# Layer A of a hybrid conv/attention trunk: a staging tile in two buffers, one column copied on another engine, one running sum begun without a copy

## The chip, the cores and the metric

The kernel runs on one core of one Trainium2 chip. The metric is the device time of one execution in microseconds; the time given for a kernel is the median of several runs. The engines of the core are TensorE (PE, with its weight loads shown as PEld), VectorE (DVE), ScalarE (ACT), GpSimd (POOL) and SyncE (SP, which issues the DMAs here). Each works through its own queue in order and waits for the others by semaphores.

## What is computed

Two layers over 1024 tokens of width 1024, in fp32, with 256 memory tokens. Layer A, which the change touches, mixes by a causal convolution of 31 taps over 1536 channels with a layer norm over the channels; layer B mixes by sparse attention. Both have a four-head cross-attention into the memory, a SiLU gate over everything and one output projection.

```python
def conformer_conv(u, conv_w, conv_b, g, b):
    a, gl = jnp.split(u, 2, axis=-1)
    h = a * jax.nn.sigmoid(gl)
    h = causal_depthwise_conv(h, conv_w) + conv_b          # 31 taps, 1536 channels
    return jax.nn.silu(layer_norm(h, g, b))

def reference(x, mem, ...):
    mem_n = layer_norm(mem, mem_ln_g, mem_ln_b)
    for i in range(DEPTH):                                 # 0: layer A, 1: layer B
        ...                                                # y_mix by convolution or by attention
        y_mem = mem_cross_attention(qm, mem_n, w_mkv)      # softmax(q k^T) v, 4 heads of 128
        y = jnp.concatenate([y_mix, y_mem], axis=-1) * jax.nn.silu(gate)
        x = layer_norm(ALPHA * x + y @ w_out, pg, pb)
    return x
```

## The kernel before

Every large product is done as three matmuls on operands split into a high and a low part (`wh`, `wl`, `xhi`, `xlo`; lines 149, 151, 153 for the projections, 599 to 601 for the output projection). Channels or heads lie on the 128 partitions and the 1024 tokens along the free dimension; a projection of 128 columns is two halves of 512 tokens, each 24 matmuls into one PSUM bank. Weights come by DMA into `wr`, are rounded to `wh` by ACT (line 131), and POOL forms the rest `wl` (line 132).

Layer A is written as a list of steps: `u_conv(i)` projects two of twelve channel tiles (`u_pair`) and convolves them (`conv_pair`), `mem_prep` normalises and transposes the memory, `gate_a(i)` makes the SiLU gate of a tile, `head_a(h)` is one memory head, `k_b(h)` and `v_b(h)` prepare layer B's keys and values. Their order is u_conv(0), u_conv(2), mem_prep, gate_a(0), u_conv(4), head_a(0), and so on, with the heads and gates between the pairs of tiles; at the end come gates 2 to 7 with `k_b` and `v_b`, the channel sums, gates 8 to 11 and the output projection. A planner in the build orders the instructions of each engine: it simulates all queues and gives an engine, of what is ready, the step written first; `low(50000)` puts the convolution behind all else. What it settles is fixed in the program, so each engine later runs its queue in that order whatever the real times are.

`mem_prep` (lines 270 to 288). Two tiles `mt0`, `mt1` of 128 memory tokens take both buffers of tag `sg`. For four groups `g` of two blocks of 128 features, PE transposes a block (line 285, two transposes into one half of a PSUM tile of tag `pt`, which has two buffers), ACT brings that half into the staging tile `mf` (line 286); after both halves `split_sb` rounds `mf` to `mhi` on ACT (line 172) and POOL forms `mlo` from `mf` and `mhi` (line 173). `mf` has tag `mp` with one buffer. Gate tiles `ga` (line 321) and `msgA` have tag `sg` too, so gate 0 needs a buffer that `mt0` holds until the last transposes have read it.

`mem_scores` takes the softmax tile `pn` (line 339) under tag `mp` in layer A and under `t01`, `t11` in layer B, as the dictionaries `TA` and `TB` say; `mem_values` transposes it (line 371). `k_b` takes the raw keys and values `kvr` (written at lines 298 and 313) under `mp`, and `v_b` stores them to DRAM.

`conv_pair` (lines 414 to 431). For two channel tiles in turn, ACT writes tap 30 with the bias into `acc` (PSUM, line 419), and DVE adds the other 30 taps, each one step to the right (line 429). The last tap goes from `acc` to an SBUF tile `co` (tag `co`, four buffers) and covers columns 1 to 1023; column 0 has no such tap and is copied by ACT (line 428). `conv_stat` (lines 433 to 453) then subtracts a shift `c_sh` from the tile on POOL (line 442; for tile 0 the shift is first made by `cmean` matmuls, line 440, and ACT, line 441), and keeps two running sums over the twelve tiles, `sumd` of the values and `sumsq` of their squares: tile 0 starts them by ACT (lines 444, 445), the others add on POOL (449, 450). Matmuls with ones (`tot`, line 534) turn the sums into the mean and variance over channels.

Of the kernel before, what the change touches and what calls it, by code (L numbers as in the profile page):

```python
# [11 lines left out]
F32 = mybir.dt.float32  # L12
# [3 lines left out]
AF = mybir.ActivationFunctionType  # L16
OP = mybir.AluOpType
# [3 lines left out]
P = 128  # L21
# [3 lines left out]
NMEM = 256  # L25
# [39 lines left out]
def trunk(ctx, tc, x, mem, mem_g, mem_b, a_w_in, conv_w, conv_b, ln_g, ln_b,  # L65
          a_w_mkv, a_w_out, a_pg, a_pb, b_w_in, b_w_mkv, b_w_out, b_pg, b_pb, out, dbg=None):
    nc = tc.nc
# [147 lines left out]
    with ExitStack() as actx:  # L215
# [54 lines left out]
        def mem_prep():  # L270
            mn = []
            for t in range(2):
                mt = sgp.tile([P, T], F32, tag="sg", bufs=2, name=f"mt{t}")
                nc.sync.dma_start(mt, mem[t * P:(t + 1) * P, :])
                rs, nb = ln_stats(mt)
                nc.scalar.activation(mt, mt, AF.Identity, bias=nb, scale=rs)
                mn.append(mt)
            for g in range(4):
                o = psum_t()
                ov = o.rearrange("p (a b) -> p a b", a=2)  # L280
                mf = am.tile([P, 2, NMEM], F32, tag="mp", bufs=1, name=f"mf{g}")
                for j in range(2):
                    k = 2 * g + j
                    for t in range(2):
                        nc.tensor.transpose(ov[:, j, t * P:(t + 1) * P], mn[t][:, k * P:(k + 1) * P], ident)
                    nc.scalar.activation(mf[:, j, :], ov[:, j, :], AF.Identity, bias=chan[:, k, TAPS + 4:TAPS + 5],
                                         scale=chan[:, k, TAPS + 3:TAPS + 4])
                split_sb(mhi[:, 2 * g:2 * g + 2, :], mlo[:, 2 * g:2 * g + 2, :], mf)
# [45 lines left out]
        def mem_scores(pl, tags, q, kv, hf, banks_s):  # L334

            n = uid()
            qh, ql = q
            kh, _, kl, _ = (kv[:, i * 256:(i + 1) * 256] for i in range(4))
            pn = pl.tile([P, 4, NMEM], F32, tag=tags["p"][hf], bufs=1, name=f"mp{n}")
            mx = small.tile([P, 4], F32, tag="mx", name=f"mx{n}")  # L340
            sm = small.tile([P, 4], F32, tag="sm", name=f"sm{n}")
            ov = banks_s()
            for jj in range(2):
                for j in range(2):
                    b = hf * 4 + jj * 2 + j
                    qs = slice(b * P, (b + 1) * P)
                    nc.tensor.matmul(ov[jj][:, j, :], qh[:, qs], kh, start=True, stop=False)
                    nc.tensor.matmul(ov[jj][:, j, :], qh[:, qs], kl, start=False, stop=False)
                    nc.tensor.matmul(ov[jj][:, j, :], ql[:, qs], kh, start=False, stop=True)
                ms = mx[:, jj * 2:jj * 2 + 2]  # L350
                nc.vector.tensor_reduce(ms, ov[jj], axis=AX.X, op=OP.max)
                nc.vector.tensor_scalar(ms, ms, -SCALE, None, op0=OP.mult)
                for j in range(2):
                    i = jj * 2 + j
                    nc.scalar.activation(pn[:, i, :], ov[jj][:, j, :], AF.Exp, bias=mx[:, i:i + 1], scale=SCALE,
                                         accum_out=sm[:, i:i + 1])
            nc.vector.reciprocal(sm, sm)
            for i in range(4):
                nc.gpsimd.tensor_scalar(pn[:, i, :], pn[:, i, :], sm[:, i:i + 1], 1.0, op0=OP.mult, op1=OP.mult)
            return pn  # L360
# [53 lines left out]
        def conv_pair(hs, i0):  # L414
# [6 lines left out]
            for s in range(TAPS - 1, 0, -1):  # L421
                for i, h, acc in zip((i0, i0 + 1), hs, accs):
                    w = chan[:, i, TAPS - 1 - s:TAPS - s]
                    if s > 1:
                        dst = acc
                    else:
                        conv_out[i] = dst = co_tile(f"co{i}")
                        nc.scalar.activation(dst[:, 0:1], acc[:, 0:1], AF.Copy)
                    nc.vector.scalar_tensor_tensor(dst[:, s:], h[:, :T - s], w, acc[:, s:], op0=OP.mult, op1=OP.add)  # L429
            for i in (i0, i0 + 1):  # L430
                conv_stat(i)
# [1 line left out]
        def conv_stat(i):  # L433
# [7 lines left out]
                    nc.scalar.activation(c_sh[:, hs], o[:, hs], AF.Copy, scale=1.0 / P)  # L441
            nc.gpsimd.tensor_tensor(d, d, c_sh, op=OP.subtract)
            if i == 0:
                nc.scalar.activation(sumd, d, AF.Copy)
                nc.scalar.activation(sumsq, d, AF.Square)
            else:
                sq = hp.tile([P, T], F32, tag="sq", bufs=1, name=f"sq{i}")
                nc.scalar.activation(sq, d, AF.Square)
                nc.gpsimd.tensor_tensor(sumd, sumd, d, op=OP.add)
                nc.gpsimd.tensor_tensor(sumsq, sumsq, sq, op=OP.add)  # L450
            if i < NCONV - 4:
                d_dram[i] = dram(f"d_dram{i}")
# [3 lines left out]
        gate_dram = [dram(f"ga{i}") for i in range(NCONV)]  # L456
        kvb_dram = [dram(f"kvb{h}") for h in range(MEM_HEADS)]

        TA = {"q": ("mqh", "mql", 1), "p": ("mp", "mp"), "ph": ("mph", "mph"), "pl": ("mpl", "mpl")}

        def head_a(h):
            kv = am.tile([P, T], F32R, tag="kv", bufs=1, name=f"kva{h}")
# [11 lines left out]
        kr = [None] * MEM_HEADS  # L474

        def k_b(h):
            kr[h] = am.tile([P, 512], F32, tag="mp", bufs=1, name=f"kvr{h}")
            mem_k(b_w_mkv, h, raw=kr[h])

        def v_b(h):  # L480
# [197 lines left out]
    with ExitStack() as bctx:  # L678
# [259 lines left out]
        with ExitStack() as tctx:  # L938
# [82 lines left out]
                if j == 3:  # L1021
                    nc.sync.dma_start(yb_d[h], y)

            TB = {"q": ("qh", "ql", 2), "p": ("t01", "t11"), "ph": ("ph0", "ph1"), "pl": ("pl0", "pl1")}
            mems = {}

            def mem_in(m):
# [157 lines left out]
```

## Time and profile before

| | |
|---|---|
| median of 3 runs | 1703.69 us (1703.56 to 1705.36) |
| the profiled execution | 1702.78 us, of which the span is 1700.0 us |
| PE busy | 1646.7 us, 97% of the span, 8214 matmuls |
| DVE, ACT, POOL busy | 1148.6, 755.8, 681.0 us |
| layer A | about the first 800 us of the span |

The page gives busy time per engine and 40 slices; the views of the trace give single instructions. In a timeline row come the start, the duration, engine, line, operation, output and inputs, and in brackets the idle time of the engine ahead of it with the instruction that ended it. Matmul durations overlap: consecutive matmuls of 512 columns start 0.23 us apart although each is shown with 0.39. PEclk is the granted clock as a share of full speed, 1.00 being 2.4 GHz.

### The profile page before, as it was taken

Reading aid. Unit: us, or ns where it says so; the run is one execution under the profiler, and the core shown is the slowest. Engines: PE = TensorE matmul, PEld = TensorE weight load, DVE = VectorE, ACT = ScalarE, POOL = GpSimd, SP = SyncE. Lnnn points to the kernel's source line nnn. Section 1 sums busy time; section 2 is a strip of 40 time slices with the busy share of each in tenths; the row PEclk is TensorE's granted clock in tenths of the full one; section 3 lists DMA queues with packets and bytes.
Section 4 is the critical chain, followed back from the end, with each engine's and each line's share of the span. In section 5 each row is a group of like instructions: output and inputs, shape, how many; then the busy total and the mean of one; then the engine's idle time right before and its main releaser. Section 6 shows DMA issues by size and latency. Waiting matters only on the chain.

```text
span 1700.0 us, 22441 instructions
## 1 busy us (share of the span) xinstructions
PE 1646.7 (97%) x8214; PEld 1379.7 (81%) x8214; DVE 1148.6 (68%) x1792; ACT 755.8 (44%) x1406; POOL 681.0 (40%) x591
## 2 busy tenths in 40 slices
PE   7999999999989999999989999899999999999997
PEld 6887888888878787887867877688888989888886
DVE  3799999989997664256169999765455555535337
ACT  4334344434343542124466776355454544533221
POOL 2344554635556365234322332433232323332233
PEclk9999999999999999999999999999999999999999
DMA  5112212222235553123311323212121221146212
GB/s 184 50 56 68 87 51 87 62 75 62 87 124 158 203 165 125 49 77 103 84 44 51 100 81 94 87 44 75 51 75 52 68 69 50 69 159 238 87 44 99
DMA packets 137789, 152.69 MB, mean 90 GB/s; under 512 B 7946, under 2 KB 108298, under 8 KB 137680
## 3 DMA queue, kind: packets, MB, share of 16 engines
q1 hardware_dynamic: 137680, 151.27, 27.9%
q8 instruction: 64, 1.05, 0.2%
q14 instruction: 45, 0.37, 0.1%
HBM read 112.71 MB, written 36.70 MB: 88 GB/s over the span
## 4 chain that ended last, share of the span: by engine, by line
PE 53%; DVE 12%; ACT 3%; issue 2%; POOL 1%; DMA 0%; DVEq 0%; ACTq 0%; POOLq 0%
PE pj L149 7%; PE pj L151 7%; PE pj L153 7%; PE pj L601 5%; PE pj L599 5%; PE pj L600 5%; DVE junk L846 3%; PE pt L998 2%; DVE xs L805 2%; PE pt L599 1%; PE pt L601 1%; PE pt L600 1%; PE S L968 1%; PE S L970 1%; PE S L969 1%
## 5 line engine op out<-in xcount | busy, mean ns | idle before, releaser
L149 PE MATMUL pj<-xhi,wh 128*128 128x512 f32 (+2 forms) x1328 | 524.1, 395 | 16.5 <-ACT gB L723 10.8
L153 PE MATMUL pj<-xhi,wl 128*128 128x512 f32 (+2 forms) x1328 | 522.3, 393 | 0.0
L151 PE MATMUL pj<-xlo,wh 128*128 128x512 f32 (+2 forms) x1328 | 520.6, 392 | 0.0
L132 POOL TENSOR_TENSOR wl<-wr,wh 128x512 fp32r<-128x512 f32 x258 | 340.3, 1325 | 436.8 <-ACT wh L131 416.5
L429 DVE SCALAR_TENSOR_TENSOR acc<-h,chan,acc 128x996 f32<-128x996 f32 (+27 forms) x348 | 418.5, 1263 | 16.4 <-ACT acc L419 15.1
L149 PEld LDWEIGHTS pj<-xhi,wh 128*128 128x128 f32 (+1 forms) x1328 | 251.2, 189 | 70.5 <-ACT gB L723 11.6
L153 PEld LDWEIGHTS pj<-xhi,wl 128*128 128x128 f32 (+1 forms) x1328 | 250.5, 189 | 49.9 <-issue 0.5
L151 PEld LDWEIGHTS pj<-xlo,wh 128*128 128x128 f32 (+1 forms) x1328 | 251.2, 189 | 48.6 <-DVE xlo L169 0.8
L131 ACT ACTIVATE wh<-wr 128x512 fp32r<-128x512 f32 (+1 forms) x230 | 143.9, 629 | 309.8 <-PE pj L151 153.7
L978 POOL TENSOR_SCALAR t<-t,smB 128x128 f32<-128x128 f32 (+3 forms) x96 | 71.6, 747 | 183.1 <-DVE smB L977 88.0
L600 PE MATMUL pj<-wl,xhi 128*128 128x512 f32 x320 | 124.1, 390 | 0.0
L599 PE MATMUL pj<-wh,xhi 128*128 128x512 f32 x320 | 123.3, 390 | 0.0
L601 PE MATMUL pj<-wh,xlo 128*128 128x512 f32 x320 | 122.6, 390 | 0.0
L973 DVE CUSTOM_DVE_ANT_0 t<-S,xs 128x128 f32<-128x128 f32 (+3 forms) x96 | 70.9, 755 | 72.8 <-PE S L970 50.8
L169 DVE TENSOR_TENSOR pl<-pt,ph 128x512 fp32r<-128x512 f32 (+1 forms) x120 | 69.2, 580 | 59.4 <-ACT ph L168 58.5
L168 ACT ACTIVATE ph<-pt 128x512 fp32r<-128x512 f32 (+1 forms) x120 | 60.2, 509 | 77.9 <-PE pt L998 71.7
L976 ACT ACTIVATE t<-t,mxB 128x128 f32<-128x128 f32 (+3 forms) x96 | 74.1, 774 | 45.6 <-DVE mxB L975 45.5
L852 ACT ACTIVATE junka<-xs,cand 128x896 bf16<-128x896 f32 (+2 forms) x93 | 80.3, 864 | 28.2 <-DVE cand L877 22.9
L846 DVE TENSOR_SCALAR_CACHE_REDUCE junk<-xs,cand 128x1024 bf16<-128x1024 f32 (+2 forms) x93 | 89.9, 967 | 2.2
L600 PEld LDWEIGHTS pj<-wl,xhi 128*128 128x128 f32 x320 | 60.1, 188 | 12.9
L601 PEld LDWEIGHTS pj<-wh,xlo 128*128 128x128 f32 x320 | 60.0, 188 | 12.9
L599 PEld LDWEIGHTS pj<-wh,xhi 128*128 128x128 f32 x320 | 60.1, 188 | 12.8
(298 smaller groups left out, 2808.5 us busy)
## 6 DMA issues: line engine op xcount, KB each, us to landing
wr<-in_a_w_in_dram SPq DMA_DIRECT2D x88, 256.0 KB
wr<-in_b_w_in_dram SPq DMA_DIRECT2D x76, 256.0 KB
wr<-in_a_w_out_dram SPq DMA_DIRECT2D x32, 256.0 KB
wr<-in_b_w_out_dram SPq DMA_DIRECT2D x32, 256.0 KB
yraw<-yb SPq DMA_DIRECT2D x16, 512.0 KB
gb<-gB SPq DMA_DIRECT2D x15, 512.0 KB
yb<-yB SPq DMA_DIRECT2D x12, 512.0 KB
sgB<-gb SPq DMA_DIRECT2D x11, 512.0 KB
```

The costliest lines, as they stand in the source:

```text
L131: nc.scalar.activation(hi, raw, AF.Copy)
L132: nc.gpsimd.tensor_tensor(lo, raw, hi.bitcast(F32), op=OP.subtract)
L149: nc.tensor.matmul(o, wh, xh, start=(k == 0), stop=False)
L151: nc.tensor.matmul(o, wh, xl, start=False, stop=False)
L153: nc.tensor.matmul(o, wl, xh, start=False, stop=(k == KD - 1))
L429: nc.vector.scalar_tensor_tensor(dst[:, s:], h[:, :T - s], w, acc[:, s:], op0=OP.mult, op1=OP.add)
L599: nc.tensor.matmul(o, yh[:, k, tsl], wh, start=(k == 0), stop=False)
L600: nc.tensor.matmul(o, yh[:, k, tsl], wl, start=False, stop=False)
L601: nc.tensor.matmul(o, yl[:, k, tsl], wh, start=False, stop=(k == 3))
L846: nc.vector.tensor_scalar(j[:, :nk(b)], xs(b), th[:, i:i + 1], None, op0=op, op1=OP.add, accum_out=c[:, i:i + 1])
L852: nc.scalar.activation(j[:, :nk(b)], xs(b), AF.Sign, bias=th[:, i:i + 1], scale=-(2.0 ** 24), accum_out=c[:, i:i + 1])
L976: nc.scalar.activation(t, t, AF.Exp, bias=mx[:, e:e + 1], scale=s, accum_out=sm[:, e:e + 1])
```

## The change

The tag `mp` gets two buffers in layer A (tiles `mf`, `pn`, `kvr`); layer B's tags keep one, now named in `TB`. Column 0 of each convolved tile is copied by DVE instead of ACT. The copy of tile 0 into `sumd` is left out, and the addition of tile 1 reads tile 0's values from its own tile. The sum of squares is begun as before.

```diff
@@ mem_prep
-                mf = am.tile([P, 2, NMEM], F32, tag="mp", bufs=1, name=f"mf{g}")
+                mf = am.tile([P, 2, NMEM], F32, tag="mp", bufs=2, name=f"mf{g}")
@@ mem_scores
-            pn = pl.tile([P, 4, NMEM], F32, tag=tags["p"][hf], bufs=1, name=f"mp{n}")
+            pn = pl.tile([P, 4, NMEM], F32, tag=tags["p"][hf], bufs=tags["p"][2], name=f"mp{n}")
@@ conv_pair
-                        nc.scalar.activation(dst[:, 0:1], acc[:, 0:1], AF.Copy)
+                        nc.vector.tensor_copy(dst[:, 0:1], acc[:, 0:1])
@@ conv_stat
             if i == 0:
-                nc.scalar.activation(sumd, d, AF.Copy)
                 nc.scalar.activation(sumsq, d, AF.Square)
...
-                nc.gpsimd.tensor_tensor(sumd, sumd, d, op=OP.add)
+                nc.gpsimd.tensor_tensor(sumd, conv_out[0] if i == 1 else sumd, d, op=OP.add)
@@ layer A, layer B
-        TA = {"q": ("mqh", "mql", 1), "p": ("mp", "mp"), "ph": ("mph", "mph"), "pl": ("mpl", "mpl")}
+        TA = {"q": ("mqh", "mql", 1), "p": ("mp", "mp", 2), "ph": ("mph", "mph"), "pl": ("mpl", "mpl")}
-            TB = {"q": ("qh", "ql", 2), "p": ("t01", "t11"), "ph": ("ph0", "ph1"), "pl": ("pl0", "pl1")}
+            TB = {"q": ("qh", "ql", 2), "p": ("t01", "t11", 1), "ph": ("ph0", "ph1"), "pl": ("pl0", "pl1")}
@@ k_b
-            kr[h] = am.tile([P, 512], F32, tag="mp", bufs=1, name=f"kvr{h}")
+            kr[h] = am.tile([P, 512], F32, tag="mp", bufs=2, name=f"kvr{h}")
```

## Rows read from the trace of the kernel before

**Rows 1.** The page, part 1: busy time, share and instructions of each engine.

```profile
PE 1646.7 (97%) x8214; PEld 1379.7 (81%) x8214; DVE 1148.6 (68%) x1792; ACT 755.8 (44%) x1406; POOL 681.0 (40%) x591
```

**Rows 2.** Timeline of PE, 125.9 to 136 us.

```profile
127.27 1.13 PE L440 MATMUL cmean<-co,ones 128*128 128x512 f32 x2
130.81 0.44 PE L285 MATMUL pt<-ident,mt 128*128 128x128 f32 x2 [2.41 <-ACT co L428]
132.77 0.80 PE L149 MATMUL pj<-xhi,wh 128*128 128x512 f32 x1 [1.53 <-ACT ga L321]
```

**Rows 3.** Windows: length, busy PE, PEld, DVE, ACT, POOL; clock, DMA share, GB/s.

```profile
127.50:132.80 5.30, 1.36 (x5) 0.29 (x4) 2.43 (x3) 5.21 (x9) 3.57 (x2) 0.97 0.17 49
132.80:136.00 3.20, 3.20 (x8) 2.56 (x9) 3.13 (x4) 3.20 (x6) 2.40 (x1) 0.52 0.83 328
136.00:142.00 6.00, 6.00 (x28) 4.95 (x27) 5.29 (x6) 4.04 (x5) 5.85 (x3) 1.00 0.22 89
```

**Rows 4.** Timeline of ACT, 100 to 160 us.

```profile
114.76 0.56 ACT L286 ACTIVATE mf<-pt,chan 128x256 f32<-128x256 f32 x1
...
118.35 0.57 ACT L286 ACTIVATE mf<-pt,chan 128x256 f32<-128x256 f32 x1 [2.37 <-POOL mlo L173]
...
127.86 0.63 ACT L172 ACTIVATE mhi<-mf 128x512 fp32r<-128x512 f32 x1
...
129.06 1.21 ACT L419 ACTIVATE acc<-h,chan 128x1024 f32<-128x1024 f32 x1
130.21 0.55 ACT L286 ACTIVATE mf<-pt,chan 128x256 f32<-128x256 f32 x1
...
130.83 1.28 ACT L321 ACT_TABLE_LOAD   x1
132.12 1.09 ACT L321 ACTIVATE ga<-pj 128x512 f32<-128x512 f32 x2
...
133.54 1.07 ACT L444 ACTIVATE sumd<-co 128x1024 f32<-128x1024 f32 x1
```

**Rows 5.** PE's groups by line, 114 to 125.4 us: busy us, mean ns.

```profile
L149 PE MATMUL pj<-xhi,wh 128*128 128x512 f32 x16 | 6.4, 401 | 0.0
```

**Rows 6.** Timeline of POOL, 100 to 160 us.

```profile
117.03 1.29 POOL L173 TENSOR_TENSOR mlo<-mf,mhi 128x512 fp32r<-128x512 f32 x1
...
128.56 1.26 POOL L173 TENSOR_TENSOR mlo<-mf,mhi 128x512 fp32r<-128x512 f32 x1 [1.14 <-ACT mhi L172]
```

**Rows 7.** Timeline of PE, 488.3 to 498 us.

```profile
492.29 0.39 PE L149 MATMUL pj<-mhi,wh 128*128 128x256 f32 x1 [3.36 <-ACT ga L321]
...
495.25 1.03 PE L371 MATMUL pt<-ident,mp 128*128 128x128 f32 x8
497.62 0.39 PE L149 MATMUL pj<-mhi,wh 128*128 128x256 f32 x1 [1.34 <-ACT kvr L298]
```

**Rows 8.** Lines L428, L429: ns min/median/max, starts; L429's idle time: us, times.

```profile
L428 ACT ACTIVATE co<-acc x12: 151/165/179, 106.1 to 545.2; 128x1 f32<-128x1 f32 x12
...
  ACT co L428: 6.0, 3
```

**Rows 9.** Timeline of DVE, 480 to 484 us.

```profile
482.71 0.15 DVE L352 TENSOR_SCALAR mx<-mx 128x2 f32<-128x2 f32 x1
482.78 2.42 DVE L429 SCALAR_TENSOR_TENSOR acc<-h,chan,acc 128x998 f32<-128x998 f32 x2
```

**Rows 10.** Lines L173, L599, L449 and tile `sumd`: ns min/median/max, first and last start.

```profile
L173 POOL TENSOR_TENSOR xlo<-co,xhi x4: 2397/2410/3391, 607.2 to 616.6; 128x1024 fp32r<-128x1024 f32 x4
...
L599 PE MATMUL pt<-wh,xhi x64: 389/389/389, 652.3 to 735.9; 128*128 128x512 f32 x64
...
L449 POOL TENSOR_TENSOR sumd<-sumd,co x11: 2386/2406/2417, 137.4 to 553.1; 128x1024 f32<-128x1024 f32 x11
...
L534 PE MATMUL tot<-sumd,ones x4: 590/592/595, 558.6 to 559.9; 128*128 128x512 f32 x4
```

**Rows 11.** Timeline of ACT, 482 to 493 us.

```profile
490.34 1.28 ACT L321 ACT_TABLE_LOAD   x1
```

## The prediction

> **What bounds the kernel now.** I read the page first: TensorE (PE) is busy 1646.7 of 1700.0 us and every other engine far less [rows 1], so the number of matmuls sets the time, and a change that touches none of them can win only time in which PE stands still or runs at the low clock. Next the list of PE's waits: the largest releaser in layer A is the Silu evacuation `ga` of a gate, and PE's timeline finds it at two places, near 132 and near 492. At the first: between the end of the second pair of `cmean` matmuls (127.27 + 1.13 = 128.40) and the next projection matmul at 132.77 PE ran only two transposes [rows 2]. The windows price it: of 127.5 to 132.8 PE was busy 1.36 of 5.30 us, so 3.9 us idle; from 132.8 to 136 the granted clock is 0.52, which is the lower level of 1.2 GHz, and 8 matmuls started, where in the following 6 us at clock 1.00 28 entries stand, 0.21 us each; 3.2 - 8 x 0.21 = 1.5 us lost [rows 3]. The stall is worth 3.9 + 1.5 = 5.4 us.
>
> Who ends it? PE's last step before it, the transposes of L285 at 130.81, waited for ScalarE (ACT) [rows 2]. The row names `co` L428, which ended at the same moment, but the code gives the real reason: these transposes fill the second half of the PSUM tile whose first half the `mf` evacuation of 130.21 reads, and that ended at 130.21 + 0.55 [rows 4]. The next matmul waited for `ga`, ACT at 132.12 [rows 2, 4]. The matmuls behind `ga` were long done: the 48 of gate 0 (16 of each of three lines, of which one is shown) lie before 125.4 [rows 5]. What kept `ga` back is in the code: it writes a tile of tag `sg`, which has two buffers, and `mt0` and `mt1` hold both until the last transposes of `mem_prep`. So the Silu of gate 0 stands behind the whole chain of `mem_prep`, PE's banks behind the Silu, and this chain is what the change shortens.
>
> **The change part by part.** (1) *Two buffers for tag `mp`, in `mem_prep`.* One step of the chain is: two `mf` halves, `mhi` (0.63), `mlo` on POOL (1.29), and only then the next group's first `mf`, since it reuses the buffer. The row of 118.35 shows this wait in plain sight: ACT idle 2.37 us for `mlo`, which ran from 117.03 to 118.32 [rows 4, 6]. The wait recurs for the third group and, at the end, `mlo` 128.56 + 1.26 = 129.82 stands before the `mf` of 130.21, although there ACT itself was taken by `acc` until 129.06 + 1.21 = 130.27 [rows 4, 6]. With two buffers a group waits for the `mlo` of the group before the last. Group 1's first half can be taken at once after group 0's, and groups then go in pairs; the step from half to half inside a group stays, as the 130.81 behind 130.21 + 0.55 shows [rows 2, 4]. Each of the three hand-overs loses about 0.63 + 1.29 = 1.9 us, 5.8 us in all, of the 130.97 - 114.76 = 16.2 us that the chain takes from its restart; for the last I count half, because of `acc`, so 4.8 us. The last transposes then stand near 126 instead of 131, and `ga`, with its table load of 1.28 us, ends about 4.5 us earlier, near 128, when PE comes off `cmean` (128.40). PE should see most of the idle time gone and, with it, the stretch at half clock. I keep 1.0 us of it as a remainder (`c_sh` and `cmean` still alternate in this place) and book 5.4 - 1.0 = 4.4 us. Bounds: 0, if the new order leaves ACT's queue in front of `ga` as it is, and 5.4.
>
> The Trainium skill speaks against a part of this. PSUM - Partial Sum Buffer, section "PSUM bank collisions raise a hardware error", wants accesses of TensorE and ScalarE to one bank kept apart by a semaphore, whatever columns they touch. The trace agrees where it can be seen: the transposes of 130.81 began 0.05 us after the `mf` on the other half of their bank [rows 2, 4]. By this rule the second buffer cannot touch the step from half to half, only the hand-over between groups. ScalarE: Activation LUTs, section "What ACT_TABLE_LOAD costs", gives 1.28 us for the load and another 1.38 us of drain at each switch of tables. The row does not show the drain: the load began at 130.83 and `ga` at 132.12 [rows 4], 1.29 us. By the page's sum `ga` would end 1.4 us later and the gain would be 3.0 instead of 4.4 us; I go by the row.
>
> (2) *The same tag in the heads and in `k_b`.* Within a head the second half's softmax cannot start before the first half's transposes, because both go through the two banks of `pt` in the order of the program; the second `mp` buffer adds nothing there: 0. In `k_b(0)` it does: the evacuation L298 writes `kvr`, which takes the buffer that head 3's last softmax still holds until its transposes of 495.25 + 1.03; PE then waited 1.34 us for L298 [rows 7]. With a free buffer L298 can run when its matmuls end, about a microsecond before the transposes are through. I book 1.3 us; bounds 0 and 1.34. The pool grows by 4 KB per partition, and layer A's accumulators afterwards lie over other tiles; no wait of PE stands at their loads, so 0.
>
> (3) *Column 0 by VectorE (DVE).* ACT loses 12 instructions of 0.165 us, 2.0 us over layer A; DVE loses the waits for them, 6.0 us in three [rows 8]. DVE gains 12 small copies. The trace has none from PSUM of this size; the nearest row is the 128x2 operation at 0.15 us, whose successor began 0.07 us later [rows 9]. Between 0.07 and 0.15 each it is 0.8 to 1.8 us; I take 1.8, so DVE ends its convolution some 4 us earlier. Queued behind each copy is only the last tap, which needs the same operands. On PE this is worth nothing: the last `xlo` from the convolution is done at 616.6 + 2.4 = 619 and first read at 652.3 [rows 10]. That 33 us of cover hides the whole item; it could turn the other way by as much without being seen.
>
> (4) *Sum begun from two tiles.* One ACT copy of 1.07 us goes; it lay at 133.54, just after `ga` [rows 4], and POOL's addition is the same instruction with another operand. The buffer of tile 0 is held until that addition, far before its reuse four tiles later. On PE: 0, except that ACT's queue after the stall is 1.07 us shorter.
>
> **Sum.** 4.4 + 1.3 = 5.7 us off the profiled execution, 1702.78 - 5.7 = 1697.1. The profiled execution is 0.9 us under the median of 1703.69, so the median should come to 1698.0. After layer A nothing is altered, and its chain begins with what PE delivers, so the gain should be carried through. But the program's order is made by a planner for all engines at once, and shorter dependences in one place move instructions in others. That is the main uncertainty, and the trace of before cannot show it.
>
> **The rivals.**
> *A, the stall stays (0.20).* The planner puts `mem_prep` earlier, but `ga` stays behind `acc`, `mf`, the copy of column 0 and the table load, which fill ACT from 129.06 to 132.1. Of that queue only `mf` (0.55) and the copy (0.165) leave [rows 4, 8]. 1703.7 - 0.7, and 0 to 1.3 of part 2: 1702 to 1703. For it: ACT was busy 5.21 of the 5.30 us [rows 3]. Against it: `ga` stands late because of its tile, not for want of priority.
> *B, given back at the channel sums (0.08).* PE's `tot` matmuls stand at 558.6; the last addition to `sumd` ends at 553.1 + 2.4 = 555.5 [rows 10], 3.1 us before. If PE comes 5.7 us sooner, POOL no sooner, and the order is kept, PE waits 2.6 us there: 1700.6. Against it: DVE's earlier end helps POOL, and other gates can be put in front.
> *C, slower (0.16).* At 492.29 PE waited 3.36 us because a pair of Exp and the table load behind it stood in ACT's queue before the `ga` that frees the bank [rows 7, 11]; PE's waits in the other three heads are all smaller. Moving ACT's work by some microseconds can give them the same order. One more such place gives 3.4 back; from two on it outweighs the gain; with three: 1698.0 + 10.1 = 1708.
> *D, more (0.12).* The same lottery the other way: the wait of 3.36 us goes as well: 1694.6.
> *The forecast (0.44)*, own range 1696 to 1700.3.
>
> **How the numbers follow.** The likeliest case gives 1698. The range must reach case A above (1703) and D below (1694.6), with a microsecond or more for the run and for bounds of part 1; case C is left out but for its first step: 1693 to 1706. About 0.2% (3.4 us) is what a measurement of this kernel can tell from no change. Faster by more, below 1700.3: the forecast 0.44, D 0.12, a little of C's mixtures 0.02, so 0.58. Slower, over 1707.1: most of C, 0.14. The same: A, B and the rest, 0.28.
>
> **What would show it.** Right: the transposes L285 all done before 127, PE's wait at L149 for `ga` near 130 gone or under 1.5 us, no window near 134 with a clock of 0.5; the wait of L149 for L298 gone; `sumd` L444 and L428 gone from ACT, 12 small copies on DVE at 0.07 to 0.2 us, and DVE without waits before the last taps; PE's busy time unchanged. Wrong: a wait of over 3 us between 120 and 135 that remains or moves to `cmean`, new waits of 3 us in the heads at 190 to 500, or a different sum of waits after 640, where I count none.

## The result

The changed kernel takes 1722.8 us (median; 1719.6 to 1724.3) against 1704.5 us for the kernel before in the same comparison: a ratio of 1.0103, 95% interval 1.0085 to 1.0121. The prediction was 1698.0 us, faster. It was wrong in sign and by 25 us.

The profiled execution of the changed kernel took 1719.59 us, with a span of 1717.8. The page, part 1, answers to [rows 1]: TensorE (PE) does the same 8214 instructions and VectorE (DVE) is busy as long as before; neither work nor a new bound has come in.

```profile
PE 1654.7 (96%) x8214; PEld 1383.2 (81%) x8214; DVE 1149.2 (67%) x1804; ACT 759.5 (44%) x1397; POOL 678.2 (39%) x591
```

**The stall that the change was costed on is gone.** The timeline of PE in the changed kernel, 122 to 127 us, answers to [rows 2]; the last column is the idle time before an entry and what ended it:

```profile
123.36 0.60 PE L285 MATMUL pt<-ident,mt 128*128 128x128 f32 x4
...
124.49 1.02 PE L440 MATMUL cmean<-co,ones 128*128 128x512 f32 x2
126.31 0.50 PE L149 MATMUL pj<-xhi,wh 128*128 128x512 f32 x1 [0.79 <-ACT ga L321]
```

The last transposes of `mem_prep` stand at 123.4 to 124.0 in place of 130.81, and PE waits 0.79 us for `ga` where it waited 2.41 and 1.53. The windows over the same place, to be set beside [rows 3] (same columns):

```profile
125.90:131.20 5.30, 4.89 (x21) 4.05 (x22) 1.34 (x2) 4.62 (x8) 3.79 (x3) 1.00 0.28 107
131.20:136.00 4.80, 4.80 (x23) 3.98 (x22) 2.08 (x2) 1.70 (x2) 0.00 (x0) 1.00 0.15 46
```

The clock is 1.00 where 132.8 to 136 had 0.52.

**Where the time went.** To compare stretches I added up PE's lost time: from the start of each matmul to the start of the next, less the median of this step for the same line and shape in the same run. This counts idle time and half clock alike. It is my own sum over the trace, not a view.

| stretch, us | before | after | difference |
|---|---|---|---|
| 40 to 145 | 6.4 | 1.1 | -5.2 |
| 145 to 225 | 0.0 | 0.1 | 0 |
| 225 to 455 | 2.3 | 19.6 | +17.3 |
| 455 to 545 | 7.3 | 15.7 | +8.4 |
| 545 to 662 | 2.6 | 2.2 | -0.4 |
| behind 662 | 48.3 | 48.0 | -0.2 |

The sum is +20; the first 48 us were 1.6 us shorter in this execution (the first transposes of L285 start at 46.40, in before at 48.00), and the spans differ by 17.8. So layer A gained 5.2 us where I said, and lost 25.7 us in two later stretches where I had expected almost nothing.

**The first loss, 225 to 455.** PE's waits there in the changed kernel (total us, times, longest), and then the only line of the same view of the kernel before:

```profile
PE pj L149 <- ACT h L407: 6.5, 2, 5.3
PE pj L149 <- ACT sig L403: 5.1, 3, 1.9
PE pt L378 <- DVE mpl L169: 0.9, 2, 0.6
```

```profile
PE pj L149 <- ACT msgA L321: 1.3, 2, 1.0
```

`h` is the input of the convolution, four buffers of one tag, so tile 7 takes the buffer of tile 3. The longest wait, in the timelines of PE, ACT and DVE of the changed kernel:

```profile
257.80 0.58 PE L149 MATMUL pj<-mhi,wh 128*128 128x256 f32 x1 [5.31 <-ACT h L407]
...
257.15 1.08 ACT L407 ACTIVATE h<-pj 128x512 f32<-128x512 f32 x2 [6.20 <-DVE co L429]
...
255.84 1.27 DVE L429 SCALAR_TENSOR_TENSOR co<-h,chan,acc 128x1023 f32<-128x1023 f32 x1
...
258.48 1.27 DVE L429 SCALAR_TENSOR_TENSOR co<-h,chan,acc 128x1023 f32<-128x1023 f32 x1
```

Read from the top: PE waits because ACT must write `h` of tile 7, ACT waits because the last tap of tile 3 (255.84) still reads the buffer, and 2.6 us later tile 4 ends as well. In the kernel before tile 3 was through near 209 and tile 4 only near 287, as ACT's copies of their column 0 show, each just ahead of a last tap:

```profile
208.41 0.15 ACT L428 ACTIVATE co<-acc 128x1 f32<-128x1 f32 x1
...
286.11 0.16 ACT L428 ACTIVATE co<-acc 128x1 f32<-128x1 f32 x1
```

Why do tiles 3 and 4 end together? The timelines of PE and ACT of the changed kernel near 173:

```profile
172.84 1.02 PE L440 MATMUL cmean<-co,ones 128*128 128x512 f32 x2
...
173.90 0.60 ACT L441 ACTIVATE c_sh<-cmean 128x512 f32<-128x512 f32 x1
174.53 2.34 ACT L419 ACTIVATE acc<-h,chan 128x1024 f32<-128x1024 f32 x2
```

The second half of `cmean` stands here, 45 us later than in before (127.27 in [rows 2]). `cmean` takes one of the two PSUM buffers of tag `acc`, in which the convolution accumulates. Until `c_sh` has read it, tile 2 (begun at 132.58) is convolved alone. Then `c_sh` and the last tap of tile 2 (DVE, 174.3) set both buffers free about a microsecond apart (174.50 and 175.58), and tiles 3 and 4 begin side by side (the two `acc` of 174.53). DVE takes a tap of the one and a tap of the other, so both end after about 82 us. From there on the pairs are (3,4), (5,6), ..., out of step with the projections, which come as (4,5), (6,7). Two tiles side by side are no loss by themselves: the kernel before convolves (2,3) and (4,5) so, pairs that match the projections.

**The second loss, 455 to 545.** Timeline of ACT in the changed kernel, inside head 3's second softmax:

```profile
500.44 1.28 ACT L355 ACT_TABLE_LOAD   x1
501.74 0.47 ACT L355 ACTIVATE mp<-pt,mx 128x256 f32<-128x256 f32 x1
...
503.90 1.28 ACT L321 ACT_TABLE_LOAD   x1
505.20 0.60 ACT L321 ACTIVATE ga<-pj 128x512 f32<-128x512 f32 x1
...
506.90 1.28 ACT L355 ACT_TABLE_LOAD   x1
508.19 0.48 ACT L355 ACTIVATE mp<-pt,mx 128x256 f32<-128x256 f32 x1
```

In the kernel before the first Exps of the same two pairs are these, with no table load between them; [rows 11] is the load behind:

```profile
484.43 0.48 ACT L355 ACTIVATE mp<-pt,mx 128x256 f32<-128x256 f32 x1
...
489.32 0.46 ACT L355 ACTIVATE mp<-pt,mx 128x256 f32<-128x256 f32 x1
```

In the changed kernel a Silu of a gate stands between the Exp pairs, with a table load on each side; head 3's first softmax is split in the same way. The changed kernel has 8 loads in this stretch, before 4; PE's longest wait there is 4.5 us for `mp` L359, which ends this softmax.

### The profile page after: what moved, and what is told of

The parts are those of the page before. It is cut to its first block, busy times and chain, and to the rows that moved or that the text cites. A ratio compares the mean times of both kernels' runs of the same rounds, so it can differ in the third digit from the quotient of the medians.

```text
span 1717.8 us, 22451 instructions
## 1 busy us (share of the span) xinstructions
PE 1654.7 (96%) x8214; PEld 1383.2 (81%) x8214; DVE 1149.2 (67%) x1804; ACT 759.5 (44%) x1397; POOL 678.2 (39%) x591
## 4 chain that ended last, share of the span: by engine, by line
PE 54%; DVE 11%; ACT 3%; issue 2%; POOL 1%; DMA 0%; DVEq 0%; ACTq 0%; POOLq 0%
PE pj L149 7%; PE pj L151 7%; PE pj L153 7%; PE pj L598 5%; PE pj L599 5%; PE pj L600 5%; DVE junk L845 3%; PE pt L997 2%; DVE xs L804 2%; PE pt L598 2%; PE pt L600 2%; PE pt L599 2%; PE S L967 1%; PE S L968 1%; PE S L969 1%
## 5 line engine op out<-in xcount | busy, mean ns | idle before, releaser
L429 DVE SCALAR_TENSOR_TENSOR acc<-h,chan,acc 128x996 f32<-128x996 f32 (+28 forms) x348 | 423.3, 1265 | 21.6 <-ACT acc L419 18.5
L599 PE MATMUL pj<-wl,xhi 128*128 128x512 f32 x320 | 124.0, 390 | 0.0
L599 PEld LDWEIGHTS pj<-wl,xhi 128*128 128x128 f32 x320 | 60.1, 188 | 12.8
```

Source lines behind the costliest of these rows:

```text
L599: nc.tensor.matmul(o, yh[:, k, tsl], wl, start=False, stop=False)
```

## The experiments

Theory T: the second half of `cmean`, of the lowest priority of all, used PE's stall of before as its slot; without the stall it is late, and its PSUM buffer costs the 18 us. R1: the second buffer in the heads costs them. R2: the copies on DVE, or the sum, cost them. T became T2 (the phase, not the delay) and gained T3 (the table loads) on the way. The table gives all runs; "tile 3" is the time of its copy of column 0, just ahead of its last tap, "loads" are ACT's table loads from 455 to 545, and the lost times are sums as above, each from one profile. A profiled execution can lie up to 4 us off its kernel's median (e6: 1697.9 against 1702.1), and the kernels were compared with before in five groups of runs, so that differences of 1 to 3 us between two rows say little.

| kernel | lost 40-145 | tile 3 | lost 225-455 | loads | lost 455-545 | median us | ratio to before (95%) |
|---|---|---|---|---|---|---|---|
| before | 6.4 | 208 | 2.3 | 4 | 7.3 | 1704 to 1705 | |
| changed | 1.1 | 256 | 19.6 | 8 | 15.7 | 1722.8 | 1.0085 to 1.0121 |
| e1 changed, cmean first | 0.4 | 216 | 1.8 | 4 | 6.7 | 1693.8 | 0.9921 to 0.9948 |
| e2 before, half at 206 | 8.5 | 229 | 0.3 | 4 | 8.9 | 1700.9 | 0.9973 to 0.9996 |
| e3 part 1 alone | 1.2 | 254 | 18.3 | 8 | 18.2 | 1722.9 | 1.0068 to 1.0124 |
| e4 parts 3, 4 alone | 6.5 | 207 | 0.5 | 8 | 16.4 | 1709.6 | 1.0017 to 1.0038 |
| e5 cmean in `pt` | 6.9 | 221 | 2.5 | 4 | 9.1 | 1707.1 | 1.0010 to 1.0030 |
| e6 part 2 alone | 6.6 | 206 | 2.5 | 4 | 5.2 | 1702.1 | 0.9971 to 0.9995 |
| e7 before, cmean first | 9.8 | 210 | 1.5 | 6 | 12.7 | 1709.9 | 1.0010 to 1.0036 |
| e8 before, both free | 7.3 | 251 | 12.6 | 8 | 20.1 | 1724.9 | 1.0086 to 1.0139 |
| e9 changed, half at 198 | 1.2 | 242 | 12.3 | 8 | 15.6 | 1712.8 | 1.0023 to 1.0053 |
| e10 parts 1, 2, cmean first | 1.5 | 216 | 2.0 | 6 | 9.2 | 1697.1 | 0.9944 to 0.9974 |
| e11 part 1, cmean first | 1.5 | 214 | 1.7 | 6 | 11.3 | 1700.9 | 0.9971 to 0.9989 |
| e13 as e8, five `h` | 8.5 | 253 | 2.9 | 8 | 19.5 | 1715.4 | 1.0052 to 1.0082 |
| e14 as e4, Exp pairs kept | 7.4 | 209 | 0.4 | 4 | 12.3 | 1704.4 | 0.9994 to 1.0013 |
| e15 changed, Exp pairs kept | 1.2 | 257 | 21.5 | 4 | 10.3 | 1717.4 | 1.0056 to 1.0086 |

### e1: the changed kernel with cmean first

```diff
-                    nc.tensor.matmul(o[:, hs], ones, d[:, hs], start=True, stop=True)
-                    nc.scalar.activation(c_sh[:, hs], o[:, hs], AF.Copy, scale=1.0 / P)
+                    with tc.high_priority(offset=60000):
+                        nc.tensor.matmul(o[:, hs], ones, d[:, hs], start=True, stop=True)
+                        nc.scalar.activation(c_sh[:, hs], o[:, hs], AF.Copy, scale=1.0 / P)
```

> The whole change, with one thing more: the two halves of the cmean matmul and the copies of them to c_sh are given a high priority in the planner's order. Theory T (the second half of cmean, of lowest priority, used PE's stall of before as its place; with the stall gone it stands at 172.84 instead of 127.27, holds one of the two PSUM buffers of the convolution, the tiles are no longer convolved in pairs and their inputs come free late): the second half stands near 125, tiles 2 and 3 start together, and the time is that of before less the gain of the memory staging, 1704.5 - 4 to 6 = 1698 to 1701, so 22 to 25 us under the changed kernel. Rival R1 (the second buffer in the heads and the order of their softmax costs the time): within 5 us of the changed kernel, over 1717. Rival R2 (the copies on VectorE, or the sum begun from two tiles, cost it): the same, over 1717.

1693.8 us, 4 us below the range of T and faster than both kernels. PE's timeline of this run:

```profile
113.71 1.02 PE L441 MATMUL cmean<-co,ones 128*128 128x512 f32 x2
...
119.59 1.02 PE L441 MATMUL cmean<-co,ones 128*128 128x512 f32 x2
120.45 0.38 PE L285 MATMUL pt<-ident,mt 128*128 128x128 f32 x2
...
125.72 0.38 PE L285 MATMUL pt<-ident,mt 128*128 128x128 f32 x2
```

Both halves lie among the transposes, tile 2 starts at 121.6, and all four parts of the change are in this kernel. So neither the heads' buffer nor the copy nor the sum has to cost 18 us, and R1 and R2 fall as causes of the whole. The windows of 225 to 455 and 455 to 545 (columns as in [rows 3]) of the kernel before, then of the changed kernel, then of e1:

```profile
225.00:455.00 230.00, 228.75 (x1129) 192.91 (x1128) 222.09 (x222) 96.09 (x172) 113.55 (x92) 1.00 0.24 74
455.00:545.00 90.00, 84.28 (x481) 73.17 (x480) 82.89 (x80) 40.51 (x78) 53.69 (x41) 1.00 0.36 115
```

```profile
225.00:455.00 230.00, 217.50 (x1046) 181.12 (x1046) 217.46 (x224) 95.12 (x161) 120.14 (x93) 0.98 0.22 70
455.00:545.00 90.00, 81.41 (x422) 68.40 (x422) 78.94 (x80) 40.00 (x71) 44.56 (x35) 0.92 0.31 95
```

```profile
225.00:455.00 230.00, 229.31 (x1133) 193.79 (x1132) 220.55 (x224) 95.39 (x164) 121.09 (x95) 1.00 0.24 74
455.00:545.00 90.00, 86.73 (x478) 74.83 (x477) 86.75 (x83) 38.93 (x75) 51.43 (x41) 0.98 0.45 147
```

PE's 11 us of missing busy time between 225 and 455 are back, and so is the granted clock (0.98 to 1.00, 0.92 to 0.98).

### e2, e8, e9: the second half of cmean late

The matmul of `hf = 1` is made to wait for a later one. In e2 and e9 that is a transpose of head 0's values; in e8 it is the last matmul of tile 5's second sigmoid gate, and the half has high priority, so that it runs there at once.

```diff
-                    nc.tensor.matmul(o[:, hs], ones, d[:, hs], start=True, stop=True)
+                    late_mm.append(nc.tensor.matmul(o[:, hs], ones, d[:, hs], start=True, stop=True))
...
+    tc.add_manual_dep(late_mm[1].ins, step.ins.name, ...)   # step: the later matmul
```

> The kernel before, without any part of the change; only the second half of cmean has to wait for the transposes of head 0's values, which is about where the changed kernel has it (172.84). Theory T: this delay alone gives the loss: the changed kernel's 18 us plus the 4 to 6 us that the staging gained there and not here, 1704.5 + 18 to 24 = 1722 to 1729; waits for h at L407 and for sig at L403 as in the changed kernel. Rivals R1 and R2: the half is needed by nobody for long, the time stays within 3 us of before, 1703 to 1708.

1700.9 us, below even what the rivals gave: T as it stood falls. Here the half stands at 206, later than in the changed kernel, tile 3 runs alone from 175 to 207, ends at 229, and PE has no wait at all between 225 and 455. A late half alone is harmless. In the changed kernel it comes at the worst moment: when the other buffer comes free too. That is T2, and e8 rebuilds that moment with nothing of the change in it.

> The kernel before, without any part of the change; the second half of cmean has to wait for the last matmul of tile 5's second sigmoid gate, and is then taken at once, so that its PSUM buffer comes free (near 174) at the same moment as the one of tile 2. The delay alone, to 206, cost nothing in the run before this one, so theory T as it stood has fallen. Theory T2: not the delay costs the time but the phase that it leaves. Where both buffers come free together, tiles 3 and 4 are convolved side by side and end together near 256 (tile 3 ended at 208.4 before), so the h buffer that tile 7 needs comes free some 47 us later than before, and after that each odd tile's; PE then waits for h and sig and drops to half clock behind each wait. T2 expects the changed kernel's loss here, 1714 to 1726, with tile 3's last tap at 245 to 260 and waits at L407 or L403. Rival R3 (the phase is harmless; the loss comes from the change's other parts in that phase): 1700 to 1707.

1724.9 us, the loss of the whole change. `c_sh` ends at 172.6 and tile 2 near 175; tile 3 starts at 172.67, tile 4 at 177.31. PE's three longest waits of five from 225 to 455:

```profile
PE pj L157 <- ACT sig L413: 3.3, 2, 1.9
PE pj L157 <- ACT co L438: 1.4, 1, 1.4
PE pj L157 <- ACT h L417: 1.1, 1, 1.1
```

R3 falls: no other part of the change is needed. The waits for `sig` and `h` are on the lines of the changed kernel (numbered ten higher here), though smaller; `co` L438 is the copy of column 0, which ACT still does here.

> The whole change; the second half of cmean still later, behind the transposes of head 0's values near 205 (it stands at 172.84 in the changed kernel). Theory T2: its PSUM buffer now comes free when tile 3 is half done, tile 4 starts half a tile behind tile 3, each h buffer comes free by itself, and the loss goes although the half stands later than ever: 1694 to 1704. Theory T (the later, the worse): 1723 or more. Rivals R1 to R3 (the change's other parts): over 1714.

1712.8 us, 10 us better with the half 26 us later, but 9 us above the upper end of what T2 expected. Its buffer came free at 200.1, not at 207.6 as in e2, because the transposes that it waits for came earlier; tile 4 then started beside the second half of tile 3, which was through at 242 and not at 229. The stretch from 225 to 455 still loses 12.3 us, and the 8 table loads are there too. In the column "tile 3" it falls in line: through by 229, the stretch loses 0.3 to 2.5 us; at 242 and 251, 12; at 254 to 257, 18 to 22 (e13, with five `h` buffers, apart).

### e13: the same phase with five h buffers

```diff
-            h = hp.tile([P, T], F32, tag="h", bufs=4, name=f"h{i}")
+            h = hp.tile([P, T], F32, tag="h", bufs=5, name=f"h{i}")
```

> The run with the kernel before and the second half of cmean late, so that tiles 3 and 4 are convolved side by side (1724.9), with one thing more: five buffers of tag h in place of four. Theory T2's link from the side-by-side convolution to PE is the h buffer that comes free late. If so, the waits at h and sig between 225 and 455 go, and with them the 10 us or so that this stretch lost against before (12.6 us of extra time between PE's starts there, 2.3 in before): 1708 to 1717, the rest of the loss, between 455 and 545, remaining. If h is not the link: 1721 or more.

1715.4 us, in the range. Tile 3 is as late as in e3 (253), and yet the stretch loses 2.9 us. Of PE's waits from 225 to 455 one line is left, with no `h` or `sig` in it:

```profile
PE pj L157 <- ACT msgA L329: 1.9, 2, 1.2
```

So the link from the phase to PE is the `h` buffer. The second stretch keeps its 19.5 us: it hangs on something else.

### e3, e4, e6: the parts one by one

```diff
 e3
-                mf = am.tile([P, 2, NMEM], F32, tag="mp", bufs=1, name=f"mf{g}")
+                mf = am.tile([P, 2, NMEM], F32, tag="mf", bufs=2, name=f"mf{g}")
 e4
-                        nc.scalar.activation(dst[:, 0:1], acc[:, 0:1], AF.Copy)
+                        nc.vector.tensor_copy(dst[:, 0:1], acc[:, 0:1])
...
-                nc.scalar.activation(sumd, d, AF.Copy)
...
-                nc.gpsimd.tensor_tensor(sumd, sumd, d, op=OP.add)
+                nc.gpsimd.tensor_tensor(sumd, conv_out[0] if i == 1 else sumd, d, op=OP.add)
 e6
-                mf = am.tile([P, 2, NMEM], F32, tag="mp", bufs=1, name=f"mf{g}")
+                mf = am.tile([P, 2, NMEM], F32, tag="mph", bufs=1, name=f"mf{g}")
...
-            kr[h] = am.tile([P, 512], F32, tag="mp", bufs=1, name=f"kvr{h}")
+            kr[h] = am.tile([P, 512], F32, tag="mp", bufs=2, name=f"kvr{h}")
```

In e6 the softmax tile gets two buffers as well, as in the change, and `mf` uses the single buffer of tag `mph`, which the heads need only later.

> The kernel before with part 1 of the change alone: the memory staging tile in two buffers of its own; the heads keep one buffer, column 0 stays on ScalarE, the sum as before. T2: the stall at 127.8 goes, the second half of cmean goes to 172 to 175, tiles 3 and 4 run side by side: 1714 to 1726, most of the whole change's loss. R1 and R2 (the heads' buffer, the copy or the sum): 1698 to 1703, the prediction's step (1) undisturbed.

1722.9 us: the part that I had costed at a gain of 4.4 us loses by itself as much as the whole change.

> The kernel before with parts 3 and 4 of the change alone: column 0 copied by VectorE, the sum begun from tiles 0 and 1. Theory T and the prediction (both parts are worth nothing on PE): within 2 us of before, 1702.5 to 1706.5, cmean's second half near 127, tiles in pairs, the waits of the last tap for column 0 (6.0 us in three) gone from VectorE. Rival R2: most of the loss is here, 1714 or more.

1709.6 us, 4.6 us slower (1.0027), where the prediction and T expected no change. The copies do what was said: the waits for column 0 are gone, and the last tile's copy stands at 541.6 in place of 545.2; 1.1 us of that was there at the first tile already (105.0 and 106.1), so 2.5 us are the copies' own. The loss lies between 455 and 545, with 8 table loads. In ACT's timeline of e4:

```profile
485.26 1.28 ACT L355 ACT_TABLE_LOAD   x1
...
488.72 1.28 ACT L321 ACT_TABLE_LOAD   x1
...
492.98 1.28 ACT L355 ACT_TABLE_LOAD   x1
```

> The kernel before with the second buffer in the heads and in k_b alone: the memory staging keeps one buffer of its own, as before. The prediction's step (2): 1.3 us off, 1703.2, bounds 0 and 1.34, the wait of 1.34 us for L298 gone. Theory T: no loss from it, 1702 to 1706. Rival R1: the loss is here, 1714 or more.

1702.1 us, 2.9 us faster (0.9983; 0.9 to 4.9 us): in T's range, and by the median more than the 1.34 us that bounded step (2). PE's two longest waits from 455 to 545 in e6:

```profile
PE pj L149 <- ACT kvr L298: 1.3, 1, 1.3
PE pj L149 <- ACT ga L321: 0.5, 1, 0.5
```

A wait for L298 of the same length is still there, but for another tile. The first of the four L298 (the keys of `k_b(0)`) in the kernel before, and then the first two of e6 with PE's wait:

```profile
497.18 0.39 ACT L298 ACTIVATE kvr<-pj 128x256 f32<-128x256 f32 x1
```

```profile
483.33 0.38 ACT L298 ACTIVATE kvr<-pj 128x256 f32<-128x256 f32 x1
...
496.59 0.39 ACT L298 ACTIVATE kvr<-pj 128x256 f32<-128x256 f32 x1
...
497.03 0.50 PE L149 MATMUL pj<-xhi,wh 128*128 128x512 f32 x1 [1.34 <-ACT kvr L298]
```

The first key tile no longer waits for head 3's last softmax. The second now takes that softmax's buffer (its transposes L371 end at 495.69), and PE waits for it. The gain is in the other wait: the 3.36 us for `ga` in [rows 7] have shrunk to 0.5. Tag `pj` has two banks, and the first key projection, whose matmuls had ended by 474.2 in before, held one of them until L298 had read it at 497.6. In e6 it is free from 483.7, and PE runs a memory projection from 486.77 to 489.81; in before it stood still from 488.93 to 492.29.

### e7, e10, e11: what each part is worth with cmean first

The edit of e1 on the kernel before (e7), on parts 1 and 2 (e10), on part 1 (e11, `mf` as in e3).

> The kernel before with the high priority for cmean and c_sh alone, none of the change. It is the control for the run in which the whole change with this priority came to 1693.8. T2: the priority by itself gives little, since the stall of the memory staging stays: 1700 to 1706. If it gives 1694 to 1697, that run's gain was the priority's and not the change's.

1709.9 us, 4 us above the range: the priority alone makes the kernel slower. The halves now lie in front of a staging chain that still stalls (9.8 us up to 145, 3.4 more than before), and between 455 and 545 there are 6 table loads and 5.4 us more. So the gain of e1 is not the priority's alone; it takes the priority and the change together.

> Part 1 alone with cmean first. Against the run with cmean first alone (1709.9, where 9.8 us of extra time between PE's starts lie between 40 and 145), the staging's second buffer should take nearly all of that: 1700.6, and 1696 to 1705 with what the heads' order adds or takes between 455 and 545. If the staging's buffer is worth less than 4 us where nothing else moves: over 1706.

1700.9 us, as expected: 9.0 us under e7 by the medians, 7.3 by the ratios to before, and 8.3 by the lost time up to 145 (9.8 to 1.5).

> Parts 1 and 2 of the change with cmean first, parts 3 and 4 left as before (column 0 on ScalarE, the sum with its copy). Compared with the whole change with cmean first (1693.8). Parts 3 and 4 alone cost 4.6 us on the kernel before. If that is a price of theirs, this run is 4 to 5 us faster, 1688.5 to 1690. If it was an accident of the order in head 3 (an Exp pair behind a table load), as T2 has it, the two agree within that accident: 1690 to 1698, and the waits of the last tap for column 0 cost PE nothing.

1697.1 us. Without parts 3 and 4 the kernel is 3.3 us slower than e1 (the two intervals just overlap), not 4 to 5 faster. What e4 lost is no fixed price of the copy or of the sum; it goes with the order in head 3.

### e5: cmean in another bank

```diff
-                o = psb.tile([P, T], F32, tag="acc", bufs=2, name="cmean")
...
+                    o = psum_t()
...
```

`psum_t()` gives each half a tile of its own.

> The whole change, with cmean's two halves in the single-bank PSUM tiles of tag pt, not in one of the two acc buffers of the convolution. T2: the convolution's buffers no longer depend on cmean, tiles 2 and 3 run side by side as before, the loss goes: 1693 to 1703, the upper end if the memory staging now waits for cmean's banks. If the loss came from where cmean stands on PE or from c_sh, and not from its PSUM buffer: 1710 or more.

1707.1 us, 4 us above the range, though the loss between 225 and 455 is gone (2.5), as T2 has it. The staging's transposes use the same banks and now lie behind both halves, at 123 to 130; the old stall is back (6.9).

### e14, e15: the Exp pairs kept together

Three Silus (both of gate 2, the second of gate 3) are ordered behind the second Exp pair of head 3's first or second softmax (6 and 7 in the edit), as they stand in the kernel before.

```diff
+        behind = {(2, 0): 6, (2, 1): 6, (3, 1): 7}
...
+                if (gate, hf) in behind:
+                    tc.add_manual_dep(s.ins, exps[behind[gate, hf]].ins.name, ...)   # s: the gate's Silu
```

> Parts 3 and 4 alone (1709.6), with the Silus of gates 2 and 3 ordered behind the second Exp pair of head 3's first and second half, as they stand in the kernel before. Theory T3: the four more table loads between 455 and 545 (8 in place of 4), each in front of an Exp or of a Silu that frees a bank, are what parts 3 and 4 cost: with 4 loads the extra time of that stretch falls from 16.4 to 6 to 9 us, and the time to 1700 to 1703. Rival: the loads go with the loss but don't make it (VectorE's taps in front of the maxima do): 1707 or more, with 4 loads.

1704.4 us, 1.4 above the range and under the rival's 1707. The loss of e4 against before is gone (1.0004, 0.9994 to 1.0013), but the stretch still loses 12.3, not 6 to 9. PE's largest wait in it shows why:

```profile
PE pj L149 <- ACT ga L324: 5.7, 2, 5.0
```

With the Exp pairs first, the gate's bank is freed late. What was won at the softmax is in part paid at the gate.

> The whole change, with the same order of Silus and Exp pairs in head 3. T3 and T2 together: the stretch from 455 to 545 loses 6 to 9 us in place of 15.7, the stretch from 225 to 455 keeps its 19.6, since tiles 3 and 4 still run side by side: 1722.8 - 7 to 9 = 1713.5 to 1716. Rival: 1720 or more.

1717.4 us, 5.3 us under the changed kernel, 1.4 short of the range for the same reason; the stretch from 225 to 455 keeps its loss (21.5). So of the 18 us about 5 come back with the order of the table loads. Most of what is left lies in the stretch that e13 ties to the convolution's phase.

## Why the prediction was wrong

**What bounds the kernel**: right. Only time in which PE stands still or runs at low clock has moved.

**Step (1), the staging chain**: right in its mechanism and nearly in its size where it acts. Forecast: the last transposes near 126, 4.4 us won with 5.4 as the bound; measured: 124, and 5.2 us. e11 against e7 gives 7 to 9 us for a chain that stalls longer. Of the drain weighed there: in the changed kernel too a table load and the instruction behind it start 1.30 us apart (500.44 and 501.74), so going by the row was right. The Trainium skill, ScalarE: Activation LUTs, section "What ACT_TABLE_LOAD costs", has 1.28 us for the load and 1.38 us of drain; the 1.30 us leave no room for the drain there.

**The step that failed** is in the reading under "What bounds the kernel now", and step (1) took it over: I took the second `cmean` pair at 127.27 as the fixed left edge of the stall (PE "comes off `cmean` (128.40)") and counted its remainder as 1.0 us. But in [rows 2] it is what filled the hole. It belongs to `low(50000)`, and in the program PE comes to it only where nothing written earlier was ready; there was such a moment because the chain held the gate's banks. By closing the hole the change took away the slot, and what the late instruction holds (a PSUM buffer that the convolution needs) was nowhere in the sum. Measured, the stretch from 225 to 455 lost 17.3 us more than in before; e8 has the whole loss in time with nothing but the half moved to the bad moment, and e1 has none of it with the half early. The prediction's own sign of being wrong came with it: a new wait of over 3 us in a head, the 5.31 us at 257.80. The text named a re-ordering by the planner as the main uncertainty and held that the trace cannot show it. For this piece it could: a row of low-priority work inside the stall, and the tag of its tile. Part of why it came late can be read too. ACT's first copy to `c_sh` in the kernel before, then in the changed one:

```profile
126.63 0.59 ACT L441 ACTIVATE c_sh<-cmean 128x512 f32<-128x512 f32 x1
```

```profile
128.64 0.60 ACT L441 ACTIVATE c_sh<-cmean 128x512 f32<-128x512 f32 x1
```

The second half writes the same PSUM tile and waits for this copy: in before it starts at 127.27, 0.05 us after the copy's end at 127.22. (In e5, with a tile for each half, PE starts both in a row, before the first copy ends at 123.03:)

```profile
121.37 1.88 PE L440 MATMUL pt<-co,ones 128*128 128x512 f32 x4
```

In the changed kernel the copy is done only at 129.24, behind both Silus of the gate. PE's wait near the old stall had ended at 126.31, and until 225 it has no other. Why the half then stands at 172.84 and not elsewhere in this full stretch the traces don't show.

**Step (2), the heads and `k_b`**: right about the tile, wrong about the wait. The key tile of `k_b(0)` no longer waits for the softmax, but the next one does, and the wait for L298 stayed (1.3 in e6, 1.2 in the changed kernel). The part alone is worth 2.9 us (0.9 to 4.9). The trace of e6 puts it in the 3.36 us wait: I took the matmuls in front of L298 for the ones that end near 495.4, but those of `k_b(0)` were done by 474.2, and with one of the two `pj` banks held PE had no work while ACT did its Exps. That is read from the code and from the order in e6; no run frees this bank alone. For the second buffer in the heads themselves no run shows a gain.

**Step (3), column 0 on DVE**: the price is in the forecast's bounds, at the lower one: a copy is shown with 0.14 to 0.16 us, but the last tap behind it starts 0.06 to 0.08 us after it (forecast 0.07 to 0.15, with 0.15 taken). In e4 the convolution's last copy gained 2.5 us, forecast 4. Its worth on PE was put at zero with 33 us of cover, and the cover is right for the convolution's end. What it doesn't cover is head 3, which shares DVE and ACT. **Step (4)** can't be told from (3): they were run together.

**Rival C** named the right place and kind: an Exp pair and a table load ahead of the Silu that frees a bank, in the heads. It was priced at 3.4 us each and 1708 with three. The second stretch did lose 8.4 us, and parts 3 and 4 alone, which lose there only, come to 1709.6. C is the smaller half of the loss: with it alone and the 5.2 us gained the time would be 1704.5 + 8.4 - 5.2 = 1707.7. **Rival A** fell (the stall went), **B** is not seen (the stretch from 545 to 662 is unchanged), and **D**, the lottery the other way, is what e1, another kernel, drew: 1693.8, with the 3.36 us wait gone.

**The range** 1693 to 1706 left out a case that is not a lottery of waits: a lasting change of phase between two engines, here worth 17 us.

**Open**: why the loads in head 3 are 4, 6 or 8. The count follows the lost time (4 loads: 5 to 9 us in the five kernels without an order written for head 3; 6: 9 to 13; 8: 16 to 20), and forcing 4 gives back about 5 us, not all. What makes the planner part the Exp pairs was not tried.

## What to carry to other kernels

Before you book the closing of a stall, list what ran inside it and at its edges: work of low priority stands there because of the stall, and when the stall goes it moves to the next hole, with every buffer that it holds. Give such work its own place by priority first; here one priority turned 18 us lost into 11 us won. And with few buffers ask not only when each comes free but which come free together: two that do can lock two pieces of work into step, and where these pairs are not the ones in which the inputs are made, the one behind them gets its buffer a whole piece late.

## What was not expected of the hardware

What surprised me is how much more than its own length a wait can cost. The windows behind the 5.31 us wait of the changed kernel (columns as in [rows 3]):

```profile
257.80:259.80 2.00, 2.00 (x9) 2.00 (x10) 1.91 (x4) 1.73 (x3) 2.00 (x2) 0.50 0.00 0
259.80:261.80 2.00, 2.00 (x11) 2.00 (x10) 1.96 (x2) 2.00 (x3) 2.00 (x2) 0.50 0.66 262
261.80:263.80 2.00, 2.00 (x12) 1.82 (x12) 2.00 (x3) 1.39 (x3) 2.00 (x2) 0.85 0.00 0
```

PE was busy without a gap and yet at 1.2 GHz, the lower of its two levels, for more than 4 us after it had stood still. Its matmuls of 256 columns follow each other there at 0.21 us, and at 0.12 us from 262.4 on. Between 225 and 455 PE's named waits come to 12.5 us, its lost time to 19.6. Of the other 7 us two stretches at half clock hold 3.7: this one, about 2.1, and one behind a wait of 1.85 us that ended at 333.61:

```profile
334.20:337.40 3.20, 3.20 (x9) 2.48 (x8) 2.57 (x4) 0.00 (x0) 0.00 (x0) 0.50 0.30 87
```

The rest are steps of up to 0.2 us over the median at full clock. The five other waits of the stretch, one of them 1.85 us too, have no half clock behind them. In the prediction I had added 1.5 us of this kind to one stall, and none to the stalls of the rivals.
